# Eight column pairs by seven products instead of five, with low halves made by an adding DMA queue

## The chip, the cores and the metric

The kernel runs on one core of one Trainium2 chip. The metric is the device time of one execution in microseconds (us). A core has TensorE (PE, matrix products; PEld is its loading of weights, which overlaps), VectorE (DVE), ScalarE (ACT), GpSimd (POOL) and SyncE (SP), each with its own list of instructions that it works off in order, and 16 DMA engines that the engines' queues feed. Data are worked on in SBUF (on-chip memory) and products are gathered in PSUM banks.

## The reference

One layer over a sequence of 512 frames of width 1024, in fp32: attention in two branches, a gated mix, and a gated feed-forward layer with a convolution. The change touches only the last:

```python
def conv_glu(x, w_up, conv_w, conv_b, w_down):
    hid = x @ w_up                                  # (512 x 1024) @ (1024 x 5632)
    hid = depthwise_causal_conv(hid, conv_w) + conv_b   # width 3, per column
    gate, up = hid[..., :D_FF], hid[..., D_FF:]     # D_FF = 2816
    return (jax.nn.silu(gate) * up) @ w_down        # (512 x 2816) @ (2816 x 1024)
...
    x = x + mixed @ w_out[l]
    x = x + conv_glu(rms_norm(x, norm2_g[l]), w_ffn_up[l], ffn_conv_w[l], ffn_conv_b[l], w_ffn_down[l])
```

## The kernel before

**High and low halves.** TensorE takes rounded fp32 (type fp32r) here. Each operand is therefore split: ACT copies it into a rounded tile, the high half, and DVE subtracts that from the source, which gives the low half. A product is three matmuls: high by high, high by low, low by high.

**The up projection.** The 2816 gate columns and the 2816 up columns go in 22 *column pairs* `up0` to `up21`: 128 gate columns and the 128 up columns that they gate, 1024 KB of weights each (tile `raw_up`). `run_chunk` runs one pair's matmuls and, at each `yield` between them, one step of the split of the next pair's weights (`split_gen`). At the end of that split stands the load two pairs ahead, on SP's queue. The order of one engine's instructions is set by a scheduler; the function `behind` fixes an order by hand where one is wanted.

An ordinary column pair (`up_body`) is 48 matmuls with 512 columns of tokens. A *seven-product pair* (`up_seven`; the set `SEVEN`, five pairs before) sees the weights as 2 by 2 blocks (gate or up, upper or lower half of the 1024 inputs) and the tokens as 2 by 2 blocks too (left or right half of the sequence), and makes 7 products of such blocks where 8 would be needed: 84 matmuls with 256 columns. It needs sums of weight blocks (`block_sums`, DVE, in tile `sx`), their high and low halves (tiles `wxh`, `wxl`; `split_seven`), and sums of token blocks, which are made once and kept in the four buffers `ts`. Products are put together on DVE and ACT in tiles `hg`, `hu` and `pc`.

After its matmuls, a pair goes through the convolution (`conv`: one ACT instruction, two DVE ones, L851 to L854), the gate (tile `cg`) and the multiplication (L928), which leaves 128 rows of hidden values in `ub`. `ub` has four slots, one for each of four consecutive pairs.

**The operands of the down projection.** It also goes by seven products, over *operand pairs*: hidden rows of column pairs 2i and 2i+1. `pair_sums(i)` makes the sums of blocks (tile `st`, one buffer, and in place in `ub`), then `halves` rounds (L908) and subtracts (L909) them into `ax{i}` (four blocks, high and low, 128x2048) and `ay{i}` (three blocks, 128x1536). Operand pairs 0 to 8 are made inside the up projection, right after the second column pair of each. The `ax` stay in SBUF (eight buffers, pair 8 in a `ts` buffer). The `ay` of pairs 0 to 6 are written to device memory (`ayd`, L933) and read back (`fetch`, L953), both by POOL's DMA queue: five reads after column pair 18, two more in the first steps of the down projection.

**The down projection.** Two passes. The first (`dn0`, 11 steps, one per operand pair) makes products 1, 2, 5 and 7 with 24 matmuls a step. The second (`dn1`, 9 steps) makes products 6, 3 and 4 with 18. Each step's weights come by one load (L123, 1024 KB, then 512 KB), are summed and split by DVE and ACT (`split_down`, L145 to L149), and stand in the same `raw`, `whi` and `wlo` buffers as in the up projection.

Of the kernel before, what the change touches and what calls it, by code (L numbers as in the profile page):

```python
# [8 lines left out]
F32 = mybir.dt.float32  # L9
# [53 lines left out]
SEVEN = (5, 8, 11, 14, 17)  # L63
# [3 lines left out]
def block_kernel(ctx: ExitStack, tc: tile.TileContext, x, xt, params, g2, rbx, wts, wd0, wd1, out):  # L67
# [45 lines left out]
    def load(i, parts=1):  # L113
# [6 lines left out]
        if i >= FIRST_DN:  # L120
            n = i - FIRST_DN
            if n < NP:
                SP.dma_start(raw, wd0[n])  # L123
            else:
                late["load"] = (SP.dma_start(raw[:, 0:1024], wd1[n - NP]),)
            yield
            return

        cuts = [0, *parts, 8] if isinstance(parts, tuple) else [8 * j // parts for j in range(parts + 1)]
        for a, b in zip(cuts, cuts[1:]):  # L130
            sl = slice(256 * a, 256 * b)
            SP.dma_start(raw[:, sl], wts[i, :, sl])
            yield
# [54 lines left out]
    def split_seven(i, raw, hi, lo):  # L188

        key = order[i]  # L190
# [3 lines left out]
        sx = late["sx"]  # L194
        for j, (h, l, src) in enumerate(((hi[:, 0:1024], lo[:, 0:1024], raw[:, 0:1024]),
                                         (wh[:, 0:1024], wl[:, 0:1024], sx[:, 0:1024]),
                                         (hi[:, 1024:2048], lo[:, 1024:2048], raw[:, 1024:2048]),
                                         (wh[:, 1024:1536], wl[:, 1024:1536], sx[:, 1024:1536]))):
            A.copy(h, src)
            V.tensor_tensor(l, src, h.bitcast(F32), op=ALU.subtract)  # L200
            if j < 3:
                yield
# [62 lines left out]
    ayd = dram.tile([7, P, 1536], F32, tag="ayd", name="ayd")  # L265

# [354 lines left out]

    def soft_b(h, t, ps):
# [247 lines left out]
    def pair_sums(i):  # L870
# [5 lines left out]
        if i < 8:  # L876
            ax = fp.tile([P, 2048], F32R, tag="ax", name=f"ax{i}", bufs=8)
            ay = fp.tile([P, 1536], F32R, tag="ay", name=f"ay{i}")
        elif i == 8:

            ax = fp.tile([P, 2048], F32R, tag="ts", name=f"ax{i}", bufs=4)
            ay = fp.tile([P, 1600], F32R, tag="wxh", name=f"ay{i}")[:, 0:1536]
            keep[0] = fp.tile([P, S], F32, tag="hg", name="t2_0")
# [367 lines left out]
```

## Time and profile before

| what | value |
|---|---|
| time, 3 runs | 726.23 us median, 725.83 to 727.21 |
| profiled execution: its own time | 726.66 us |
| profiled execution: span from first to last instruction | 724.9 us |
| TensorE clock granted | 1.000 |
| bytes moved by DMA | 100.91 MB, 139 GB/s |
| up projection with what follows, until the down matmuls | 360.00 to 615.80 us: PE 255.80 busy, DVE 214.60, ACT 138.99 |
| down projection | 615.80 to 724.90 us: PE 104.91 busy, DVE 89.27, ACT 45.90 |

In the rows of groups and of the chain, "L998" is a line of the program, then come the engine, the operation, the written tile, "<-", the tiles read, and "x84" the number of instructions. In a table of stretches each row has its window in us, its length, and busy us with counts for PE, PEld, DVE, ACT and POOL. In the rows of DMA issues the last number is the median time from issue to landing in us. SPq and POOLq are the queues that SP and POOL feed.

### The profile page before, as it was taken

Reading aid. Unit: us, or ns where it says so; the run is one execution under the profiler, and the core shown is the slowest. Engines: PE = TensorE matmul, PEld = TensorE weight load, DVE = VectorE, ACT = ScalarE, POOL = GpSimd, SP = SyncE. Lnnn points to the kernel's source line nnn. Section 1 sums busy time; section 2 is a strip of 40 time slices with the busy share of each in tenths; the row PEclk is TensorE's granted clock in tenths of the full one; section 3 lists DMA queues with packets and bytes.
Section 4 is the critical chain, followed back from the end, with each engine's and each line's share of the span. In section 5 each row is a group of like instructions: output and inputs, shape, how many; then the busy total and the mean of one; then the engine's idle time right before and its main releaser. Section 6 shows DMA issues by size and latency. Waiting matters only on the chain.

```text
span 724.9 us, 10589 instructions
## 1 busy us (share of the span) xinstructions
PE 718.6 (99%) x4019; PEld 627.5 (87%) x4019; DVE 565.4 (78%) x1030; ACT 401.5 (55%) x727; POOL 53.6 (7%) x95
## 2 busy tenths in 40 slices
PE   8999999999999999999999999999999999999997
PEld 8999998888988888888889889889898988888886
DVE  6678867775988888566275799998979985997686
ACT  6675656657767676442254556655545653543541
POOL 2701200000101011000012000000000100000000
PEclk9999999999999999999999999999999999999999
DMA  8632232211313111314536613544335553564563
GB/s 308 250 131 78 83 117 74 74 59 58 118 63 113 59 59 59 136 68 144 195 149 239 203 62 156 186 135 160 118 145 186 181 184 117 173 243 174 177 222 116
DMA packets 24786, 100.91 MB, mean 139 GB/s; under 512 B 2592, under 2 KB 7328, under 8 KB 17184
## 3 DMA queue, kind: packets, MB, share of 16 engines
q1 hardware_dynamic: 21792, 87.00, 33.8%
q0 software_dynamic: 2656, 13.11, 5.0%
q8 instruction: 31, 0.51, 0.3%
q14 instruction: 19, 0.16, 0.1%
q10 hardware_dynamic: 288, 0.14, 0.1%
HBM read 88.44 MB, written 11.80 MB: 138 GB/s over the span
## 4 chain that ended last, share of the span: by engine, by line
PE 98%; DMA 1%; SPq 0%; DVE 0%; ACT 0%; DVEq 0%; issue 0%
PE P L1087 14%; PE p L998 7%; PE pg L254 4%; PE pg L253 4%; PE pg L255 4%; PE pu L254 4%; PE pu L255 4%; PE pu L253 4%; PE qkB L255 2%; PE gB L255 2%; PE qkB L253 2%; PE gA L253 2%; PE gA L254 2%; PE gB L253 2%; PE gA L255 2%; PE qkB L254 2%
## 5 line engine op out<-in xcount | busy, mean ns | idle before, releaser
L253 PE MATMUL pg<-hth,whi_up 128*128 128x512 f32 (+1 forms) x152 | 55.7, 367 | 0.0
L255 PE MATMUL pg<-hth,wlo_up 128*128 128x512 f32 (+1 forms) x152 | 55.7, 366 | 0.0
L254 PE MATMUL pg<-htl,whi_up 128*128 128x512 f32 (+1 forms) x152 | 55.7, 366 | 0.0
L254 PE MATMUL pu<-htl,whi_up 128*128 128x512 f32 (+1 forms) x152 | 55.6, 366 | 0.0
L253 PE MATMUL pu<-hth,whi_up 128*128 128x512 f32 (+1 forms) x152 | 55.6, 366 | 0.0
L255 PE MATMUL pu<-hth,wlo_up 128*128 128x512 f32 (+1 forms) x152 | 55.6, 365 | 0.0
L1087 PE MATMUL P<-whi_dn,ax 128*128 128x512 f32 x176 | 54.4, 389 | 0.0
L149 ACT CAST whi_dn<-raw_dn 128x1024 fp32r<-128x1024 f32 x33 | 34.3, 1051 | 25.5 <-PE P L1087 15.2
L145 DVE TENSOR_TENSOR wlo_dn<-raw_dn,whi_dn 128x1024 fp32r<-128x1024 f32 x33 | 40.0, 1224 | 9.2 <-ACT whi_dn L149 9.1
L228 DVE TENSOR_TENSOR wlo_up<-raw_up,whi_up 128x1024 fp32r<-128x1024 f32 (+1 forms) x40 | 41.2, 1062 | 7.0 <-ACT whi_up L226 7.0
L226 ACT CAST whi_up<-raw_up 128x1024 fp32r<-128x1024 f32 (+1 forms) x40 | 34.5, 917 | 14.7 <-PE pu L254 7.9
L1087 PE MATMUL P<-whi_dn,ay 128*128 128x512 f32 x132 | 40.8, 389 | 0.0
L1087 PEld LDWEIGHTS P<-whi_dn,ax 128*128 128x128 f32 x176 | 33.0, 188 | 6.8
L1087 PE MATMUL P<-wlo_dn,ax 128*128 128x512 f32 x88 | 34.2, 389 | 0.0
L254 PEld LDWEIGHTS pu<-htl,whi_up 128*128 128x128 f32 x152 | 28.6, 188 | 4.7
L253 PEld LDWEIGHTS pu<-hth,whi_up 128*128 128x128 f32 x152 | 28.5, 188 | 4.7
L255 PEld LDWEIGHTS pg<-hth,wlo_up 128*128 128x128 f32 x152 | 28.6, 188 | 4.7
L255 PEld LDWEIGHTS pu<-hth,wlo_up 128*128 128x128 f32 x152 | 28.5, 188 | 4.6
L253 PEld LDWEIGHTS pg<-hth,whi_up 128*128 128x128 f32 x152 | 28.6, 188 | 4.6
L254 PEld LDWEIGHTS pg<-htl,whi_up 128*128 128x128 f32 x152 | 28.6, 188 | 4.5
L633 DVE TENSOR_TENSOR_SCAN aB<-aB,reset 128x127 f32<-128x127 f32 (+3 forms) x32 | 26.0, 817 | 6.7 <-ACT aB L628 6.7
L1087 PEld LDWEIGHTS P<-whi_dn,ay 128*128 128x128 f32 x132 | 24.8, 188 | 5.1
(303 smaller groups left out, 2240.3 us busy)
## 6 DMA issues: line engine op xcount, KB each, us to landing
raw_up<-in_wts SPq DMA_DIRECT2D x22, 1024.0 KB, 4.8
raw_dn<-in_wd SPq DMA_DIRECT2D x11, 1024.0 KB, 4.8
raw_dn<-in_wd SPq DMA_DIRECT2D x11, 512.0 KB, 3.4
ayd<-ay POOLq DMA_DIRECT2D x7, 768.0 KB, 5.2
ay<-ayd POOLq DMA_DIRECT2D x7, 768.0 KB, 6.5
raw_gA<-in_wts SPq DMA_DIRECT2D x4, 1024.0 KB, 4.7
raw_qkB<-in_wts SPq DMA_DIRECT2D x4, 1024.0 KB, 4.8
raw_gB<-in_wts SPq DMA_DIRECT2D x4, 1024.0 KB, 4.7
```

The costliest lines, as they stand in the source:

```text
L145: chain("halves", V.tensor_tensor(o, x, y, op=op))
L149: chain("casts", A.copy(hi[:, sl], src))
L226: A.copy(hi[:, sl], raw[:, sl])
L228: E.tensor_tensor(lo[:, sl], raw[:, sl], hi[:, sl].bitcast(F32), op=ALU.subtract)
L253: PE.matmul(ps, sh, mh, start=first, stop=False)
L254: PE.matmul(ps, sh, ml, start=False, stop=False)
L255: PE.matmul(ps, sl, mh, start=False, stop=last)
L633: V.tensor_tensor_scan(ar, ar, reset[:, S - n:S - 1][:, ::-1], 1.0, op0=ALU.mult, op1=ALU.max)
L998: PE.matmul(ps, st, mv[:, k, :], start=first and k == 0 and n == 0, stop=last and k == 3 and n == 2, skip_group_check=True)
L1087: chain("products", PE.matmul(dst, st, mv, start=first and n == 0, stop=last and n == 2, skip_group_check=True))
```

## The change

1. `SEVEN` has eight pairs, 5, 8, 10, 12, 14, 16, 18 and 20, instead of 5, 8, 11, 14 and 17.
2. The block sums of a seven-product pair need one tile of their own, `s1` (128x512) instead of `sx` (128x1536); two of the sums are written over the weights they were made from. Their splitting goes in another order.
3. For operand pairs 0 to 8 the low halves are made without DVE: ACT writes the rounded value, then the negated rounded value into the low half, and a POOL DMA adds the source to it (`accum_op`), four such DMAs per operand pair.
4. The steps of `pair_sums` aren't issued at the end of the column pair but one at a time at the next yields, from the list `late["todo"]`.
5. `ay` has two buffers. Its spill goes on SP's queue, behind the latest load of weights, a period of two column pairs later than before; `ax0` is spilled too, at operand pair 6, and read back by POOL after column pair 20 into a `ts` buffer. Operand pair 8 uses the ordinary buffers `ax` and `ay`.
6. The reads of `ay` go into the down projection: after steps 0, 2, 3, 5, 6 and 8 of its first pass and after step 0 of its second. Each waits for the landing of the latest load of weights (`after`).
7. `pc` is a third as wide; two PSUM copies go into halves of `hg` and `hu` instead.

```diff
-SEVEN = (5, 8, 11, 14, 17)
+SEVEN = (5, 8, 10, 12, 14, 16, 18, 20)
...
     def block_sums(i):
         b = raws[i].rearrange("p (b c) -> p b c", c=512)
-        sx = late["pool"].tile([P, 1536], F32, tag="sx", name=f"sx_{order[i]}")
-        late["sx"] = sx
-        s1, s2, s4 = (sx[:, 512 * j:512 * (j + 1)] for j in range(3))
+        s1 = late["s1"] = late["pool"].tile([P, S], F32, tag="s1", name=f"s1_{order[i]}")
         V.tensor_tensor(s1, b[:, 1], b[:, 3], op=ALU.add)
         yield
-        V.tensor_tensor(s2, s1, b[:, 0], op=ALU.subtract)
-        yield
-        V.tensor_tensor(s4, b[:, 2], s2, op=ALU.subtract)
-        yield
         V.tensor_tensor(b[:, 1], b[:, 0], b[:, 1], op=ALU.subtract)
         yield
...
+        def part(h, l, c0, src):
+            sl = slice(c0, c0 + src.shape[-1])
+            A.copy(h[:, sl], src)
+            V.tensor_tensor(l[:, sl], src, h[:, sl].bitcast(F32), op=ALU.subtract)
+        part(hi, lo, 0, raw[:, 0:1024])
+        V.tensor_tensor(b[:, 0], s1, b[:, 0], op=ALU.subtract)
+        yield
+        part(wh, wl, 0, s1)
+        part(wh, wl, 512, b[:, 0])
+        yield
+        part(hi, lo, 1024, raw[:, 1024:2048])
+        V.tensor_tensor(b[:, 2], b[:, 2], b[:, 0], op=ALU.subtract)
+        yield
+        part(wh, wl, 1024, b[:, 2])
...
         for _ in body(*splits.pop(key)):
             next(sp, None)
+            if late.get("todo"):
+                late["todo"].pop(0)()
             yield
...
+    def after(ins, others):
+        for o in others:
+            tc.add_manual_dep(ins.ins, o.ins.name, mybir.DependencyInfo(
+                mybir.DependencyClass.Sync, mybir.DependencyReason.DATA), reason="paced")
+        return ins
...
                 A.copy(a[:, sl], src)
-                ins.append(V.tensor_tensor(a[:, n + o:n + sl.stop], src, a[:, sl].bitcast(F32), op=ALU.subtract))
+                if i < 9:
+                    A.activation(lo, src, AF.Copy, scale=-1.0)
+                    G.dma_start(lo, src, accum_op=ALU.add)
+                else:
+                    ins.append(V.tensor_tensor(lo, src, a[:, sl].bitcast(F32), op=ALU.subtract))
...
-            for step in pair_sums(j // 2):
-                step()
-            if j // 2 < 7:
-                G.dma_start(ayd[j // 2], pairs[j // 2][1].bitcast(F32))
+            i = j // 2
+            late["todo"] += pair_sums(i)
+            if 0 < i < 8:
+                late["todo"].append(lambda: behind(SP.dma_start(ayd[i - 1], pairs[i - 1][1].bitcast(F32)), late["ld"]))
+            if i == 6:
+                late["todo"].append(lambda: behind(SP.dma_start(axd, pairs[0][0].bitcast(F32)), late["ld"]))
...
-        G.dma_start(ay, ayd[i])
+        after(G.dma_start(ay, ayd[i]), late["ld"])
...
-        if j == 18:
-            for i in range(5):
-                fetch(i)
+        if j == SEVEN[-1]:
+            keep[0] = fp.tile([P, S], F32, tag="hg", name="t2_0")
+            ax0 = fp.tile([P, 2048], F32R, tag="ts", name="ax0_", bufs=4)
+            G.dma_start(ax0, axd)
+            pairs[0] = (ax0, None)
...
+            n = ({0: 0, 2: 1, 3: 5, 5: 6, 6: 2, 8: 3}, {0: 4})[s].get(i)
+            if n is not None:
+                fetch(n)
```

**How the order changes on DVE.** Before, around the splitting of seven-product pair 11 while pair 10 runs. The numbers in the names of tiles are the pair's and then the program's own; L228 is the low half of an ordinary pair's weights, L200 that of a seven-product pair's, L909 the low half of a down operand, L899 to L901 its sums, L853 a tap of the convolution.

```order
L228 TENSOR_TENSOR wlo_up10_5119<-raw_up10_4965,whi_up10_5118 128x1024
L909 TENSOR_TENSOR ay3_4972<-ub_4184,ay3_4972 128x256
L899 TENSOR_TENSOR ub_4184<-ub_4184 128x256
L900 TENSOR_TENSOR st3_4973<-st3_4973,ub_4184 128x256
L853 SCALAR_TENSOR_TENSOR cg8_5081<-hg8_4992,par_88,cg8_5081 128x511
L200 TENSOR_TENSOR wxl_up11_5209<-sx_up11_5155,wxh_up11_5208 128x1024
L909 TENSOR_TENSOR ax3_4971<-st3_4973,ax3_4971 128x256
L200 TENSOR_TENSOR wxl_up11_5209<-sx_up11_5155,wxh_up11_5208 128x512
L853 SCALAR_TENSOR_TENSOR ub_4184<-hu8_4993,par_88,ub_4184 128x511
L901 TENSOR_TENSOR st3_4973<-ub_4184,st3_4973 128x256
L909 TENSOR_TENSOR ax3_4971<-ub_4184,ax3_4971 128x768
```

Now, from the last product of seven-product pair 12, while pair 14 is split (L1037 and L1038 put products together, L906 is a sum of operand pair 5, L863 and L864 are taps, L192 a low half of pair 14's weights, L194 and L200 block sums):

```order
L1037 TENSOR_TENSOR hu12_5429<-p7_12_5425,hu12_5429 128x256
L906 TENSOR_TENSOR st5_5447<-ub_4185,st5_5447 128x256
L1038 TENSOR_TENSOR hu12_5429<-hu12_5429,pc12_5427 128x256
L863 SCALAR_TENSOR_TENSOR cg12_5538<-hg12_5428,par_88,cg12_5538 128x511
L864 SCALAR_TENSOR_TENSOR cg12_5538<-hg12_5428,par_88,cg12_5538 128x510
L192 TENSOR_TENSOR wlo_up14_5576<-raw_up14_5415,whi_up14_5575 128x1024 x2
L194 TENSOR_TENSOR raw_up14_5415<-s1_up14_5489,raw_up14_5415 128x512
L863 SCALAR_TENSOR_TENSOR ub_4185<-hu12_5429,par_88,ub_4185 128x511
L200 TENSOR_TENSOR raw_up14_5415<-raw_up14_5415 128x512
L864 SCALAR_TENSOR_TENSOR ub_4185<-hu12_5429,par_88,ub_4185 128x510
L192 TENSOR_TENSOR wxl_up14_5578<-raw_up14_5415,wxh_up14_5577 128x512
L939 TENSOR_TENSOR ub_4185<-cg12_5538,ub_4185 128x512
```

The subtractions L909 have gone from this list, and two block sums now stand inside the split, ahead of the last low half.

**On SP's queue**, which had only loads of weights in this stretch, the spills now stand between them:

```order
L129 DMA raw_up17_5684<-in_wts 128x2048
L944 DMA ayd_108<-ay5_5422 128x1536
L947 DMA axd_109<-ax0_4438 128x2048
L129 DMA raw_up18_5850<-in_wts 128x2048
L129 DMA raw_up19_5902<-in_wts 128x2048
L944 DMA ayd_108<-ay6_5639 128x1536
```

A spill follows the load of an odd pair; the next even pair's load stands behind it.

**On POOL's queue**, the end of the list now, the last additions and the reads back:

```order
L918 DMA ay8_6074<-ub_4185 128x256
L918 DMA ax8_6073<-st8_6099 128x256
L918 DMA ax8_6073<-ub_4185 128x768
L918 DMA ay8_6074<-st8_6099 128x512
L1077 DMA ax0__6407<-axd_109 128x2048
L967 DMA ay0_6530<-ayd_108 128x1536
L967 DMA ay1_6613<-ayd_108 128x1536
```

Before, the end of this list held spills and reads alone. Each operand pair now puts four additions on this queue, and the reads of `ay` come after all of them.

More of the change, by code (lines that the diff above doesn't have):

```diff
@@ L121, in load @@
             n = i - FIRST_DN
[L122 to L125, printed above, removed]
+            late["ld"] = (SP.dma_start(raw, wd0[n]) if n < NP else SP.dma_start(raw[:, 0:1024], wd1[n - NP]),)
             yield
@@ L193, in split_seven @@
         splits[key] = tuple(t.rearrange("p (k c) -> p k c", c=P) for t in (hi, lo, wh, wl))
[L194 to L202, printed above, removed]
+        b = raw.rearrange("p (b c) -> p b c", c=512)
+        s1 = late["s1"]
+        def part(h, l, c0, src):
[12 more added lines that the diff above has]
+        part(wh, wl, 1024, b[:, 2])
     def split_gen(i, pieces):
@@ L1023, in body @@
             V.tensor_tensor(hu[:, left], b7, hu[:, right], op=ALU.add)
-            V.tensor_tensor(hu[:, right], hu[:, right], pc[:, 1], op=ALU.add)
+            V.tensor_tensor(hu[:, right], hu[:, right], pc, op=ALU.add)
             up_fin(j, None, hu, g)
@@ L1050, in block_kernel @@
     late["ts"] = token_sums()
+    late["todo"] = []
     for j in range(NF):
@@ L1054, in block_kernel @@
             pass
-        if j == 18:
-            for i in range(5):
-                fetch(i)
+        if j == NF - 1:
+            for step in late["todo"]:
+                step()
+            late["todo"] = []
+        if j == SEVEN[-1]:
[3 more added lines that the diff above has]
+            pairs[0] = (ax0, None)
     BLK = {1: 0, 2: 1, 5: 2, 7: 3, 3: 0, 4: 1, 6: 2}
@@ L1179, in steps1 @@
         for t in range(NT):
-            behind(SP.dma_start(tmp["x"][t // 2][:, t % 2, :], x2d[t]), late["load"])
+            behind(SP.dma_start(tmp["x"][t // 2][:, t % 2, :], x2d[t]), late["ld"])
             if t in (1, 2):
```

29 lines of the change are left out of this document (13 added, 16 removed).

## The prediction

> **What bounds the kernel now.** I read the page's engine shares first, then the chain of work that ended last, then what TensorE waited for, then a table of stretches, then the chain in order of time.
>
> ```profile
> PE 718.6 (99%) x4019; PEld 627.5 (87%) x4019; DVE 565.4 (78%) x1030; ACT 401.5 (55%) x727; POOL 53.6 (7%) x95
> ...
> PE 98%; DMA 1%; SPq 0%; DVE 0%; ACT 0%; DVEq 0%; issue 0%
> ```
>
> PE is 99% busy and 98% of the chain. The waits of PE alone have three rows, all at the program's start; the largest is this one, and the other two are 0.6 and 0.4 us:
>
> ```profile
> PE warm L301 <- DVE warm L298: 1.1, 1, 1.1
> ```
>
> So no later PE instruction waited for data, and the end moves with the PE work, one for one, as long as the other engines keep ahead. How far ahead they are is the question of this change. The table of stretches, cut at the starts of column pairs 5, 8, 14 and 17 (each row is three column pairs; columns are us, then busy us of PE, PEld, DVE, ACT and POOL with counts, clock, DMA share, GB/s):
>
> ```profile
> 435.60:467.28 31.68, 31.68 (x182) 27.92 (x182) 31.68 (x52) 20.01 (x32) 1.07 (x2) 1.00 0.47 176
> ...
> 530.64:562.32 31.68, 31.68 (x182) 27.92 (x182) 26.39 (x41) 16.88 (x26) 1.09 (x2) 1.00 0.49 169
> ```
>
> DVE is busy all of the first stretch and 83% of the last, ACT 53 to 63%, DMA under half; PE never stops. DVE is the engine that would be next. The chain in order of time gives the price of a column pair in both forms:
>
> ```profile
> 467.28 9.89 PE p L998 x84
> 477.17 0.23 PE pg L253
> ...
> 498.96 9.89 PE p L998 x84
> ...
> 615.78 104.94 PE P L1087 x462
> ```
>
> A pair by seven products takes 9.89 us. From 477.17 to 498.96 lie two ordinary pairs: 21.79 us, 10.895 each.
>
> **The change, part by part.** *Products.* Five such pairs become eight. Each new one saves 10.895 - 9.89 = 1.005 us, three save **3.02 us**. PE's list holds nothing else new, and its clock stands at 1.00 in the rows above, so there is no other PE term; the down projection (462 matmuls from 615.78) is the same list. What remains is whether PE stays fed.
>
> *DVE.* From column pair 8 on, seven-product and ordinary pairs alternate, so the load repeats every 9.89 + 10.895 = 20.8 us, where it repeated every 31.68 us. DVE overlaps the end of one instruction with the next, so I take start to start from its timeline:
>
> ```profile
> 482.41 0.42 DVE L909 TENSOR_TENSOR ay<-ub,ay 128x256 fp32r<-128x256 f32 x1
> 482.75 0.42 DVE L899 TENSOR_TENSOR ub<-ub 128x256 f32<-128x256 f32 x1
> ...
> 487.15 0.95 DVE L909 TENSOR_TENSOR ax<-ub,ax 128x768 fp32r<-128x768 f32 x1
> 488.02 0.75 DVE L854 SCALAR_TENSOR_TENSOR cg<-hg,par,cg 128x510 f32<-128x510 f32 x1
> 488.68 0.75 DVE L854 SCALAR_TENSOR_TENSOR ub<-hu,par,ub 128x510 f32<-128x510 f32 x1
> 489.34 2.36 DVE L200 TENSOR_TENSOR wlo_up<-raw_up,whi_up 128x1024 fp32r<-128x1024 f32 x2
> 491.61 0.75 DVE L853 SCALAR_TENSOR_TENSOR ub<-pu,par,ub 128x511 f32<-128x511 f32 x1
> 492.27 0.69 DVE L909 TENSOR_TENSOR ay<-st,ay 128x512 fp32r<-128x512 f32 x1
> 492.87 0.69 DVE L928 TENSOR_TENSOR ub<-cg,ub 128x512 f32<-128x512 f32 x1
> ```
>
> That is 0.34 us at 256 elements, 0.60 at 512, 0.87 at 768, 1.135 at 1024 and 0.66 for a tap of the convolution. In the changed order one 20.8 us period has 8 taps (5.3), 4 of 1024 (4.5), 9 of 512 (5.4) and 9 of 256 (3.1): **18.3 us, 88%**. Before, 31.68 us held 12 taps, 7 of 1024, 9.5 of 512, 1.5 of 768 and 14 of 256: 27.6 us, 87%. The subtractions that leave (0.34 + 0.34 + 0.87 + 0.60 = 2.15 us for each of nine operand pairs) pay for the denser sevens. DVE is no fuller than now, with 2.5 us free in each period.
>
> *Time of a split.* Whether it is also in time: seven-pair 14 is split while 13 runs. By the order shown, after pair 12's last product (call this 0) DVE has the last two 256s, two taps, two 1024s, 512, tap, 512, tap and then 512 four times: 8.6 us. Its handovers with ACT, which rounds the same pieces first, I put at 0.5 to 1 us (the new ACT row of pair sums stands between), so the last low half is ready at about +9.4. PE starts 14 at +10.9 and wants that third only in the sixth product, 5 x 1.41 us later, at +17.9; the first pieces are ready at +5 and wanted at +10.9. Cover: 6 us or more; a delay of DVE up to that costs nothing. The load of the weights of 16 is issued when 14 is split (+9.4), lands 4.8 us later (below) at +14.2, and DVE comes to its first sum at about +15, behind the split of 15, which waits for PE to leave 13 at +10.9. If the load is late by 3 us, DVE idles 2 of its 2.5 free us and PE notices nothing.
>
> *ACT.* It gets a second pass over each operand (scale -1), for which there is no row; the rounding of the same piece is the nearest (groups of ACT in one stretch of the old kernel, each row one shape: busy us, mean ns):
>
> ```profile
> L908 ACT CAST ax<-ub 128x768 fp32r<-128x768 f32 x2 | 1.7, 840 | 0.6 <-DVE ub L899 0.6
> ...
> L908 ACT CAST ay<-st 128x512 fp32r<-128x512 f32 x2 | 1.3, 626 | 0.0
> L851 ACT ACTIVATE ub<-hu,par 128x512 f32<-128x512 f32 x1 | 0.8, 821 | 0.0
> L908 ACT CAST ay<-ub 128x256 fp32r<-128x256 f32 x2 | 0.8, 410 | 0.0
> L908 ACT CAST ax<-st 128x256 fp32r<-128x256 f32 x2 | 0.8, 405 | 0.0
> ```
>
> Between 0.84 + 0.63 + 0.41 + 0.41 = 2.3 us a period (as a cast) and 3.0 (stretched by 821/626, as an activation with pointer operands). I take 2.3, the same pieces. Three shorter roundings and four copies of a seven every 20.8 instead of 31.68 us raise the rest: 53% become about 67%. Hidden under PE; uncovered it would be 2.3 us x 9 = 21 us.
>
> *The adding queue.* Four POOL DMAs per operand pair (128, 128, 384, 256 KB) add the source to the negated high half. No row has such an addition; plain transfers and POOL's own time for one are the nearest rows:
>
> ```profile
> raw_up<-in_wts SPq DMA_DIRECT2D x22, 1024.0 KB, 4.8
> ayd<-ay POOLq DMA_DIRECT2D x7, 768.0 KB, 5.2
> ay<-ayd POOLq DMA_DIRECT2D x7, 768.0 KB, 6.5
> ...
> htd<-xf_n POOLq DMA_DIRECT2D x8, 256.0 KB, 3.3
> ...
> L933 POOL DMA_DIRECT2D ayd<-ay x7 | 3.7, 535 | 134.0 <-DVE ay L909 73.9 <-DVE cg L853 45.9 <-DVE pc L1010 14.2
> ```
>
> POOL pays 0.54 us each and is idle otherwise. An addition takes between 3.3 us (a copy) and twice that, 6.6 (the destination is read too). The last of four is issued when ACT has negated its piece, at about +5.5; the next pair's sums overwrite its source (`st`, one buffer) at about 20.8 - 1.1 = +19.7. Cover 14 us, so I take zero at both ends. Behind a late one stand DVE's sums and then every split; that is rival 1. The Trainium skill (Collectives: The Full Stack, "The bandwidth ceiling: the fold count and why AG ≠ RS ≠ AR") says that an add inside the DMA path costs nothing by its arithmetic but reads two sources, and gives a ratio of 1.93. By it an addition would be 6.4 us by estimate and the sum the same 3.02 us; no run here shows one yet.
>
> *Spills.* They move from POOL to SP, right behind the load of an odd pair's weights, and wait there for additions that were issued a period earlier. Behind a waiting spill stand the loads; by the above there is no wait. Seven of 768 KB and one of 1024 KB in 180 us, 0.47 DMA share at most: hidden. The next user of an `ay` buffer comes 20 us after its spill.
>
> *Fetches.* Five of seven came before the down projection; now the first operand (1024 KB) comes during column pair 21 and six of seven fetches in the first pass, each behind the landing of a load, which is just before the next load is issued. What that does to a load, two places show, with opposite answers (first pair of rows 574 to 580 us, second 631 to 634 us):
>
> ```profile
> ay<-ayd POOLq DMA_DIRECT2D x2, 768.0 KB, 9.0
> raw_up<-in_wts SPq DMA_DIRECT2D x1, 1024.0 KB, 8.8
> ...
> raw_dn<-in_wd SPq DMA_DIRECT2D x1, 1024.0 KB, 4.7
> ay<-ayd POOLq DMA_DIRECT2D x1, 768.0 KB, 7.6
> ```
>
> Behind several fetches the load took 8.8 us, with one fetch issued just after it 4.7: between 0 and 4.0 us more. The tightest use is the load for down step 6:
>
> ```profile
> 637.72 0.33 SPq L123 DMA_DIRECT2D raw_dn<-in_wd  x1
> ...
> 644.73 1.41 DVE L145 TENSOR_TENSOR raw_dn<-raw_dn 128x512 f32<-128x512 f32 x2
> 646.06 2.43 DVE L145 TENSOR_TENSOR wlo_dn<-raw_dn,whi_dn 128x1024 fp32r<-128x1024 f32 x2
> ```
>
> It lands at 637.72 + 4.8 = 642.5, DVE starts on it at 644.73, the first low half is there at about 647.3, and PE comes to it at 615.78 + 6 x 5.45 = 648.5 (24 of the 462 matmuls at 0.227 us are a step). Cover 2.2 + 1.2 = 3.4 us; one fetch beside it I put at up to 2 us, so zero. The Trainium skill (DMA: Bandwidth & Descriptors, "Issuing engines are not separate DMA queues") says that all issuers' transfers interleave on the same 16 engines. By it each load beside a fetch would be slowed, by estimate 1.7 us, still inside the cover; the 8.8 us row agrees and the 4.7 us row does not.
>
> *Sum:* the profiled execution took 726.66 us with a span of 724.9, so 1.76 us lie around it. 726.66 - 3.02 = 723.64; the median of the runs, 726.23, is 0.43 below the profiled one, which makes **723.2**.
>
> **The rivals.** *1. The queue of additions is the bound (slower).* If four additions run one after another, each twice a copy (2 x (3.3 + 3.3 + 3.8 + 3.3) = 27 us, the 384 KB put between the 3.3 and 5.2 rows), a pair takes 27 us of a 20.8 us period. It decides from 20.8 us a pair. `st` is then freed 6.6 us later each time; DVE's 2.5 and PE's 6 us are used up in the first two pairs, and some five pairs remain: 5 x 6.6 - 2 = +31, about 754 us. For it: nothing here shows an addition. Against: three fetches of 768 KB in a row landed in 6.5 to 9.0 us, so transfers of this queue overlap.
>
> *2. Fetches starve the first down pass.* If loads of steps 6, 7, 9 and 10 all take 8.8 us, step 6 is 0.6 us late at PE, step 7 about 1, step 9, which waits for step 7's buffer, 2 to 3: some 4 us, 727 us with the gain in it; half of that gives 725.2. For: the 8.8 us row. Against: that load stood behind four fetches, here there is one.
>
> *3. DVE and ACT are too entangled in the alternating stretch.* Six periods that each run 0.5 us over take the gain back: 726.2. For: the stretch from 435.60, where DVE had no gap at all. Against: PE was fed even there, and the load a period is no larger.
>
> **How the numbers follow.** Forecast 0.72, rival 1 0.07, rival 2 0.12, rival 3 0.09. The likeliest case by itself lies between 722.5 and 724.6. With most of rivals 2 and 3 the range is 722.4 to 726.6; rival 1 is left out. A measurement of this kernel tells 0.2%, 1.5 us, from no change. Faster by more: 0.72 and a small part of 2 and 3, 0.74. Within: the middle of 2 and 3, 0.14. Slower: rival 1 and the far end of 2, 0.12.
>
> **What would show it.** Right: eight stretches of 84 seven-product matmuls of 9.89 us, PE's waits still only at the start, DVE near 88% between column pairs 8 and 20, additions landing within 14 us. Wrong: a PE row waiting for `wlo` or `wxl` in the up projection with DVE waiting for a DMA at the pair sums (rival 1), PE waiting for `wlo_dn` in steps 5 to 10 with loads above 7 us (rival 2), PE waiting behind DVE with no DMA late (rival 3). A seven that takes longer than 9.89 us when it follows an ordinary pair each time would make the gain itself too large.

## The result, and the profile after

The changed kernel takes **731.39 us** (median of 11 runs, 727.48 to 735.97) against 726.14 us before: 1.007 times the time, 95% interval 1.005 to 1.009. It is slower, where 723.2 and faster was forecast. Its runs also lie further apart than those of before (8.5 us against 1.7 us).

The engines' shares and the chain of waits, from the page of the changed kernel:

```profile
PE 718.4 (99%) x4127; PEld 631.6 (87%) x4127; DVE 566.4 (78%) x1035; ACT 427.2 (59%) x789; POOL 81.8 (11%) x125
...
PE 87%; DVE 5%; issue 3%; DMA 2%; ACT 2%; POOL 0%; SPq 0%; DVEq 0%; ACTq 0%; POOLq 0%
```

The chain was 98% PE before. Now 13% of it is something else. What PE waited for (us in total, times, longest):

```profile
PE pg L255 <- DVE cg L864: 1.7, 1, 1.7
PE qA L382 <- ACT whi_qA L226: 1.7, 1, 1.7
PE warm L304 <- DVE warm L301: 1.1, 1, 1.1
PE p L1012 <- ACT hg L1017: 1.0, 1, 1.0
```

The second and third are at the program's start. The first and last are new and lie together, around 475 us, inside column pair 8. The table of stretches shows what follows them (us, then busy us of PE, PEld, DVE, ACT, POOL, granted clock, DMA share, GB/s):

```profile
460.00:480.00 20.00, 17.24 (x98) 15.12 (x97) 15.81 (x24) 13.87 (x24) 3.44 (x4) 0.89 0.67 178
480.00:500.00 20.00, 20.00 (x119) 18.18 (x119) 18.04 (x30) 14.19 (x24) 3.46 (x4) 0.94 0.62 173
477.00:619.00 142.00, 141.96 (x875) 128.57 (x875) 125.57 (x202) 92.77 (x158) 21.29 (x25) 0.98 0.66 189
```

PE stands still for 2.7 us, and around the second gap the clock goes to half for a while: (0.11 + 0.06) x 20 = 3.4 us of clock lost. From 477 us on, DVE is at 125.57 / 142 = 88% and ACT at 65%, as forecast (88 and 67), and PE hardly stops. So one place makes the loss: 726.66 - 3.02 + 2.7 + 3.4 = 729.7 us, and the profiled execution took 729.98. The 3.4 is a little too much, because the half clock begins inside the second gap, where PE does nothing anyway; the matmuls behind it lose 2.9 us (below), and with that some 0.7 us stay unexplained.

The chain in order of time leads back from that place (start, us, what; "issue" is time in which the engine waited for nothing that the profile shows):

```profile
443.36 0.29 POOL ay L918
443.65 7.51 issue
...
451.17 0.86 POOL ax L918
452.03 2.07 issue
454.11 0.85 POOL ax L918
454.96 3.55 issue
458.53 3.93 DMA ay<-st
...
462.58 0.44 DVE st L903
...
465.24 0.95 ACT whi_up L191
...
473.09 1.72 ACT whi_up L226 x2
...
476.26 0.27 ACT hg L1017
476.58 7.17 PE p L1012 x36
```

The part shown begins with the four additions (L918) of operand pair 1. The next pair's first sum (L903) waits for the last of them to land, because it overwrites the tile `st` that the addition reads. Behind that sum, in DVE's and ACT's lists, stand the split of column pair 8 (L191), the rounding of pair 9 (L226) and the copy (L1017) that PE needs for the second half of pair 8. The 36 matmuls after it take 7.17 us, where 36 of an uninterrupted pair take 36 / 84 x 9.89 = 4.24: that is the half clock.

The additions don't overlap. From the records of issue and landing in the changed kernel's trace (us):

| addition | issued | landed | next one issued |
|---|---|---|---|
| ay<-ub, pair 1 | 443.36 | 450.86 | 451.17 |
| ax<-st | 451.17 | 453.80 | 454.11 |
| ax<-ub | 454.11 | 458.22 | 458.53 |
| ay<-st | 458.53 | 462.46 | 462.77 |

Of all 36, not one was issued before the one ahead of it had landed, and 29 of the 35 that follow another were issued 0.31 to 0.35 us after it. One takes 2.6 to 7.6 us, 4.4 on average, so an operand pair's four, from the first issue to the last landing, take 16 to 24 us, 18.6 on average. The program does not ask for this order: none of the semaphore waits that the trace records ahead of these 35 is for the addition before.

### The profile page after: what moved, and what is told of

It is laid out like the page before. It is cut to its first block, busy times and chain, and to the rows that moved or that the text cites. A ratio compares the mean times of both kernels' runs of the same rounds, so it can differ in the third digit from the quotient of the medians.

```text
span 728.2 us, 11018 instructions
## 1 busy us (share of the span) xinstructions
PE 718.4 (99%) x4127; PEld 631.6 (87%) x4127; DVE 566.4 (78%) x1035; ACT 427.2 (59%) x789; POOL 81.8 (11%) x125
## 3 DMA queue, kind: packets, MB, share of 16 engines
q0 software_dynamic: 6976, 16.91, 10.1%
## 4 chain that ended last, share of the span: by engine, by line
PE 87%; DVE 5%; issue 3%; DMA 2%; ACT 2%; POOL 0%; SPq 0%; DVEq 0%; ACTq 0%; POOLq 0%
PE P L1108 14%; PE p L1012 9%; PE pu L255 2%; PE pg L257 2%; PE pu L256 2%; PE pg L255 2%; PE pg L256 2%; PE pu L257 2%; PE qkB L257 2%; PE qkB L255 2%; PE gB L257 2%; PE gA L255 2%; PE gA L256 2%; PE gB L255 2%; PE gA L257 2%
## 5 line engine op out<-in xcount | busy, mean ns | idle before, releaser
L146 ACT CAST whi_dn<-raw_dn 128x1024 fp32r<-128x1024 f32 x33 | 34.5, 1051 | 27.5 <-DMA raw_dn<-in_wd 13.7
L255 PE MATMUL pg<-hth,whi_up 128*128 128x512 f32 (+1 forms) x128 | 46.5, 363 | 1.7 <-DVE cg L864 1.7
L257 PE MATMUL pg<-hth,wlo_up 128*128 128x512 f32 (+1 forms) x128 | 46.4, 362 | 0.0
L256 PE MATMUL pg<-htl,whi_up 128*128 128x512 f32 (+1 forms) x128 | 46.3, 362 | 0.0
L256 PE MATMUL pu<-htl,whi_up 128*128 128x512 f32 (+1 forms) x128 | 46.3, 362 | 0.0
L255 PE MATMUL pu<-hth,whi_up 128*128 128x512 f32 (+1 forms) x128 | 46.3, 362 | 0.0
L257 PE MATMUL pu<-hth,wlo_up 128*128 128x512 f32 (+1 forms) x128 | 46.2, 361 | 0.0
L228 DVE TENSOR_TENSOR wlo_up<-raw_up,whi_up 128x1024 fp32r<-128x1024 f32 (+1 forms) x34 | 33.6, 1030 | 4.2 <-ACT whi_up L226 4.1
L226 ACT CAST whi_up<-raw_up 128x1024 fp32r<-128x1024 f32 (+1 forms) x34 | 28.6, 893 | 9.9 <-PE pu L256 6.3
L645 POOL TENSOR_SCALAR_AFFINE_SELECT bB<-bB 128x128 f32<-128x128 f32 x32 | 13.6, 429 | 149.2 <-DVE bB L644 135.9
L674 ACT CAST pth_A<-pT_A 128x128 fp32r<-128x128 f32 (+2 forms) x40 | 14.6, 371 | 22.4 <-PE pT_A L661 14.7
```

Of the source, the lines that this page charges most:

```text
L146: chain("casts", A.copy(hi[:, sl], src))
L226: A.copy(hi[:, sl], raw[:, sl])
L228: E.tensor_tensor(lo[:, sl], raw[:, sl], hi[:, sl].bitcast(F32), op=ALU.subtract)
L255: PE.matmul(ps, sh, mh, start=first, stop=False)
L256: PE.matmul(ps, sh, ml, start=False, stop=False)
L257: PE.matmul(ps, sl, mh, start=False, stop=last)
```

## The experiments

What follows from each is read from the stages of its profiled execution:

| run | last matmul of kA at | pair 5 to down projection | down projection, first to last matmul | that execution, us | median us |
|---|---|---|---|---|---|
| before | 72.1 | 180.2 | 104.7 | 726.66 | 726.1 |
| changed | 72.0 | 183.5 | 104.8 | 729.98 | 731.4 |
| x9: changed again | 73.8 | 183.1 | 105.1 | 731.64 | 731.6 (one run) |
| x1: copies for additions | 73.9 | 177.0 | 105.7 | 726.33 | 725.9 |
| x2: 8 additions a pair | 72.4 | 260.0 | 104.8 | 806.93 | 812.7 |
| x3: spill behind the load | 72.2 | 189.2 | 105.1 | 736.07 | 733.4 |
| x4: DVE for pairs 0 to 2 | 72.3 | 178.2 | 104.8 | 725.06 | 728.5 |
| x5: five sevens | 71.6 | 185.7 | 105.7 | 732.69 | 733.6 |
| x6: no additions | 73.5 | 178.0 | 107.3 | 728.50 | 727.7 |
| x7: 2 additions | 74.2 | 177.3 | 106.9 | 728.51 | 726.1 |
| x8: 1 addition | 74.1 | 177.8 | 104.8 | 726.78 | 726.7 |
| x10: before, more memory | 71.4 | 180.2 | 104.7 | 725.90 | 725.9 (one run) |
| x11: order of pairs | 73.8 | 184.7 | 104.8 | 733.08 | 730.7 |
| x12: 2 additions, late fetches | 72.5 | 177.3 | 111.2 | 731.17 | 731.2 |
| x13: before, longer list | 72.8 | 199.2 | 104.7 | 751.86 | 751.9 (one run) |
| x14: 2 additions, even fetches | 72.6 | 177.3 | 105.0 | 724.98 | 725.2 |
| x15: as x14, five sevens | 71.6 | 180.2 | 104.7 | 726.75 | 727.2 |

`kA` is the second projection at the start of the program; a matmul counts from its start. "Pair 5" is the first matmul of column pair 5, the first seven-product pair. The profiled execution is not always a typical one: of x2, x4 and x5 it was the fastest, of x3, x7 and x11 the slowest.

The sum expected 180.2 - 3.0 = 177.2 us for the second stage and no change in the others.

### Is it the adding? Copies in its place (x1)

```diff
-                    G.dma_start(lo, src, accum_op=ALU.add)
+                    G.dma_start(lo.bitcast(F32), src)
```

> The changed kernel with the 36 additions turned into plain copies of the same source to the same place on the same queue; the low halves of the down operands then hold the source itself, so the subtraction is left out. The order of TensorE's and the other engines' lists is the same as in the changed kernel. Theory A (an adding DMA is issued only once the addition before it has landed, so four of them take 15 to 22 us a pair and hold the sums and the spills): copies go out 0.5 to 1 us after one another, no wait of DVE for the tile st, TensorE without a gap in column pair 8, 723 to 724 us. Theory B (DVE and ACT are too full and too entangled around column pairs 5 to 8, whatever the queue does): the gap of 2.7 us in pair 8 and the half clock stay, 730 to 732 us.

Measured 725.86 us (724.12 to 727.59), ratio 0.9997 (0.9987 to 1.0007), and the second stage took 177.0 us without a gap. POOL's timeline in this kernel, pair 1:

```profile
444.56 0.54 POOL L918 DMA_DIRECT2D ay<-ub  x1 [10.01 <-DVE hu L1027]
445.22 0.54 POOL L918 DMA_DIRECT2D ax<-st  x1
447.39 0.55 POOL L918 DMA_DIRECT2D ax<-ub  x1 [1.64 <-DVE hg L1033]
450.87 0.54 POOL L918 DMA_DIRECT2D ay<-st  x1 [2.93 <-ACT whi_up L226]
```

The second copy goes out 0.66 us after the first, each takes POOL 0.54 us (an addition 0.86), and from the first issue of four to the last pass 6.3 us, where the additions took 15.2. With the bytes (16.91 MB on this queue), the lists and the spills the same, the gap of pair 8 and the half clock behind it are gone. (The copies also go in fewer packets, 4096 on the queue instead of 6976.) Theory A holds for the stage; the total, 2 us over its forecast, has the two other losses in it that the table shows, one at the start and one in the down projection.

### Twice as many additions (x2)

```diff
-                    G.dma_start(lo, src, accum_op=ALU.add)
+                    h = src.shape[-1] // 2
+                    for q in (slice(0, h), slice(h, 2 * h)):
+                        G.dma_start(lo[:, q], src[:, q], accum_op=ALU.add)
```

> The changed kernel with each addition cut in two halves of the columns, 8 per operand pair; bytes, sums and the order of TensorE's list stay. Theory A: each of the eight takes 2.9 us or more from issue to issue, 24 to 35 us a pair where a period has 20.8, so the queue becomes the bound from the third pair on and the time goes to 745 to 790 us. Theory B: the queue overlaps its transfers and only 36 more issues of 0.9 us are added on POOL, 729 to 733 us.

Measured 812.69 us, ratio 1.118 (1.113 to 1.123): beyond even theory A's range. All 71 that follow another were issued within 0.35 us after its landing, and DVE's waits are the rival's of the prediction, grown large:

```profile
DVE st L903 <- DMA ay<-st: 71.0, 7, 13.9
```

The range was passed because PE, starved pair after pair, also ran 65 us at half clock in that execution.

### Which wait, the spill's or the sums'? (x3, x4)

x3 lets the first spill stand behind the load of column pair 8 on SP:

```diff
             if 0 < i < 8:
+                late["todo"] += [lambda: None] * 2
                 late["todo"].append(lambda: behind(SP.dma_start(ayd[i - 1], ...), late["ld"]))
```

> The changed kernel with the spill of each ay issued two steps later, so that on SP's queue the first spill stands behind the load of column pair 8 instead of ahead of it; the other spills stand where they stood and TensorE's list is the same. Theory A1 (the load of pair 8 is late because the spill ahead of it waits for the last addition of operand pair 0): the load is issued about 2 us earlier and lands 3 to 4 us earlier, DVE's 4.5 us wait for it goes, the gap in pair 8 shrinks below 1 us and the clock stays full: 723 to 726 us. Theory A2 (the wait for the tile st, 2.6 us, makes the gap by itself): the load comes earlier and the gap of 2 to 3 us in pair 8 stays, 729 to 731 us. Theory B: as A2.

Measured 733.42 us, ratio 1.0095 (1.0063 to 1.0127). The load did go out at 439.5 us instead of 443.5, and the stall stayed; three more gaps came between 563 and 587 us. A1 falls. A2's mechanism stands, though the time is above its 729 to 731: in this execution, 736.07 and the slowest of five, DVE waited 18.7 us in all for `st`, against 9.3 in the changed kernel. In x4, which follows, SP still waited 27.5 us for additions ahead of spills, with a second stage of 178.2 us; that wait costs little.

```diff
-                if i < 9:
+                if 3 <= i < 9:
```

> The changed kernel with the low halves of operand pairs 0, 1 and 2 made by DVE subtractions as before, additions only for pairs 3 to 8. Theory A: the pile of additions behind pair 0 is gone, the first spill and the load of pair 8 don't wait, no gap in pair 8 and the additions of pairs 3 to 8 just fit their period: 723 to 725 us. Theory B: DVE gets 2.15 us more for each of three pairs in the stretch where it is too full already, so the gap grows: 731 to 735 us.

Measured 728.53 us (725.06 to 730.45), ratio 1.0026 (1.0007 to 1.0044). The median lies in neither theory's range. In the profiled execution, the fastest at 725.06, the stage is 1 us over the sum, so there the pile behind pairs 0 and 1 was nearly all of the loss. The runs spread over 5.4 us, and by the medians (731.4 in the changed kernel, 728.5 here) only about half of the loss to the forecast of 723.2 went away. That with four additions a pair the other places still go wrong in some executions is likely and not shown, since the one trace is of the fastest.

### Is it the number of sevens, or DVE? (x5, x6)

```diff
-SEVEN = (5, 8, 10, 12, 14, 16, 18, 20)
+SEVEN = (5, 8, 11, 14, 17)
```

> The changed kernel with the old five seven-product pairs (5, 8, 11, 14, 17); additions, spills, fetches and block sums as changed. Theory A (the additions run one at a time, some 18 us an operand pair, and make the loss by themselves): the gap around column pair 8 stays as it stands behind pairs 0 and 1, which are the same here, and the 3.02 us of three sevens are missing: 731 to 736 us. Theory B (it is the eight sevens with their block sums that overfill DVE and ACT): five of them go back to a fed TensorE, 726 to 728 us.

Measured 733.58 us, ratio 1.0104 (1.0084 to 1.0123). With the old set the same two waits stand in the same place, 473 to 477 us:

```profile
PE pg L255 <- DVE cg L864: 1.7, 1, 1.7
...
PE p L1012 <- ACT hg L1017: 1.0, 1, 1.0
```

Theory B falls: the eight sevens are not what makes the loss.

```diff
-                if i < 9:
-                    A.activation(lo, src, AF.Copy, scale=-1.0)
-                    G.dma_start(lo, src, accum_op=ALU.add)
+                if False:
+                    pass
                 else:
                     ins.append(V.tensor_tensor(lo, src, a[:, sl].bitcast(F32), op=ALU.subtract))
```

> The changed kernel with all low halves made by DVE subtractions, no addition on the queue; eight sevens, spills on SP and fetches as changed. DVE gets 2.15 us more a period: 18.3 + 2.15 = 20.5 of 20.8 us. Theory A: no wait for the tile st and no spill that waits for an addition; DVE is at 98 percent and falls behind a little only, 723 to 727 us. Theory B: DVE over its limit, gaps in every second pair, 732 us or more.

Measured 727.71 us, ratio 1.0025 (1.0015 to 1.0035). Its row for the stretch with the alternating pairs:

```profile
477.00:619.00 142.00, 141.07 (x869) 126.66 (x867) 136.11 (x224) 86.00 (x137) 0.55 (x1) 1.00 0.39 138
```

DVE is at 96% without additions, and PE still loses only 0.9 us there. The total is 0.7 us over theory A's range, and most of it lies at the start and in the down projection, where PE waited 1.1 us for DVE's last tap (L864) and 0.7 us for a low half.

### Fewer additions (x7, x8)

```diff
-                if i < 9:
+                if i < 9 and o == 0:                 # x7: the two pieces from ub
+                if i < 9 and o == 0 and n == 1024:   # x8: the piece of 768 columns alone
```

> The changed kernel with only the two pieces that come from ub (768 and 256 columns) made by additions; the two from the tile st go to DVE as before (0.34 + 0.60 = 0.94 us a pair). Theory A: two additions take 7 to 11 us a pair, the tile st is free as soon as DVE is done, spills wait little: TensorE is fed from column pair 5 to 21, 177 us for that stretch, 722.5 to 724.5 us. Theory B (additions in any number disturb the loads, or DVE is too full): 728 us or more.

> As the one with two additions, but only the piece of 768 columns is made by an addition, 1.28 us more on DVE a pair than in the changed kernel (19.6 of 20.8 us). Theory A: as with two, 722.5 to 724.5 us, with the spills, which hold only ay, never waiting for an addition. Theory B: DVE at 94 percent shows gaps, 726 us or more.

Measured 726.12 us, ratio 0.9998 (0.9988 to 1.0009), and 726.72 us, ratio 1.0002 (0.9992 to 1.0011): no change, and both miss theory A's 722.5 to 724.5 us. With two, the second stage is 177.28 us, so the three sevens pay 2.9 of the 3.02 us; the profiled execution lost 2.1 us at the start and 2.2 us in the down projection. It was the slowest of ten, 728.51, so the median has only a part of these losses. PE's waits in it:

```profile
PE qA L382 <- ACT whi_qA L226: 2.0, 1, 2.0
PE warm L304 <- DVE warm L301: 1.1, 1, 1.1
PE P L1108 <- DVE wlo_dn L142: 0.9, 1, 0.9
```

The last one is step 10 of the first down pass. Its load took 8.1 us beside the fetch of `ay2` and 8.4 us for that: the prediction's rival 2, which had this load among the slow ones but counted its delay at steps 6, 7 and 9. With one addition the time fits theory B's 726 us or more, but not for its reason: the second stage is 177.8 us with one gap of 0.4 us, and a start 2 us later than before takes the rest.

### The same kernel again, and the order of the pairs (x9, x11)

> The changed kernel once more, for a second trace. Theory A (additions one at a time, at the edge of their 20.8 us period): the gaps of TensorE between column pairs 5 and 21 come again, in pair 8 or where the queue happened to be late, and the stretch takes 180 to 190 us instead of the 177.2 of the sum; the first additions again leave 0.3 us after the landing of the one before. If TensorE's 1.7 us gap at 6.7 us of the program belongs to the kernel, it is there again; if it is chance, it is between 0.4 and 1.7.

The changed kernel's second trace: 731.64 us, 183.1 us in the second stage, PE gaps of 1.1 and 0.8 us at the start of pair 8 and 0.3 and 1.0 us in its middle, and 29 additions again issued within 0.35 us after a landing. The stall came again, so it belongs to the kernel. The start was 1.7 us later than in its first trace, behind a gap of 2.7 us.

In the changed kernel's TensorE list the scheduler had put two matmuls of pair 9 into the middle of pair 8 (and of pair 17 into 16), and PE's first wait stands at one of them. TensorE's timeline at that place in the changed kernel:

```profile
472.88 0.28 PE L1012 MATMUL p<-ts,wxl_up 128*128 128x256 f32 x1
474.90 0.47 PE L255 MATMUL pg<-hth,whi_up 128*128 128x512 f32 x1 [1.74 <-DVE cg L864]
475.20 0.40 PE L256 MATMUL pg<-htl,whi_up 128*128 128x512 f32 x1
476.58 0.58 PE L1012 MATMUL p<-hth,whi_up 128*128 128x256 f32 x1 [0.97 <-ACT hg L1017]
```

x11 holds an ordinary pair's first matmul behind the last one of the seven ahead (`mm7`):

```diff
+            if k == 0 and "mm7" in late:
+                first7 = late.pop("mm7")
+                behind(PE.matmul(ps[:, c0:c1], hi[:, k, o:o + P], hth[:, k, c0:c1], start=True, stop=False), (first7,))
...
+                continue
```

> The changed kernel with the first matmul of an ordinary column pair held behind the last one of the seven-product pair ahead of it, so that the two matmuls of pair 9 no longer stand in the middle of pair 8 (nor pair 17's in 16). Theory A (the additions): DVE and ACT are late all the same and TensorE waits at the second half of pair 8 for ACT instead; 728 to 733 us. Theory C (TensorE's list is the cause): no gap in pair 8, 723 to 726 us.

Measured 730.69 us, ratio 1.0065 (1.0048 to 1.0083), and the wait is there all the same, now nearly in one piece in pair 8 (3.4 us):

```profile
PE p L1018 <- ACT hg L1023: 4.3, 3, 3.4
```

Theory C falls.

### The late start (x10, x13)

In the eleven traces with eight sevens up to x12, the second piece of the first weights landed late, and PE waited 1.7 to 2.7 us at about 6.7 us; in those of before and x5 it waited at most 1.0. x10 gives the old kernel more device memory, by two unused slots in `ayd` (1.5 MB; the changed kernel has 1 MB more than before); x13 gives it a list for TensorE as long as that of eight sevens:

```diff
+        if (c0, c1) == (0, S) and extra[0] < 108:
+            extra[0] += 4
+            for _ in range(4):
+                PE.matmul(ps[:, c0:c1], hi[:, 0, o:o + P], hth[:, 0, c0:c1], start=True, stop=True)
```

> The kernel before with two more slots in the device memory tensor ayd, which are never used, so that what lies in device memory stands as far apart as with the changed kernel's second spill tensor. If the place in memory makes the slower first loads (landing 5.8 to 6.5 us after issue instead of 4.95), this kernel shows them too and a TensorE gap of 1.7 us or more at the start; if not, gaps of 0.4 and 0.6 us and 726 us.

> The kernel before with 108 matmuls more on TensorE's list (four at the head of each half of the first ordinary column pairs, whose results are overwritten), so that the list is as long as with eight seven-product pairs (4127). They cost 108 x 0.227 = 24.5 us. If the length of TensorE's list (what has to be brought in, or where the program lies) makes the first loads late, TensorE has a gap of 1.7 us or more near 6.7 us and the last matmul of kA comes at 72.5 to 74 us; if not, gaps of at most 1.0 us in all and 71.3 to 72.1 us.

x10: 725.9 us, no wait but the 1.1 us for `warm` that every trace has, kA's last matmul at 71.4 us. x13: 751.86 us, which is 25.7 over before (24.5 for the matmuls), kA's last matmul at 72.8, and the gap is there. TensorE's timeline of before, then of x13:

```profile
7.61 0.74 PE L379 MATMUL qA<-whi_qA,hth 128*128 128x256 f32 x4 [0.59 <-ACT whi_qA L226]
```

```profile
9.21 0.74 PE L379 MATMUL qA<-whi_qA,hth 128*128 128x256 f32 x4 [2.47 <-ACT whi_qA L226]
```

TensorE's list in x13 differs from before's only from 403 us on. Over all traces, the 13 with 4127 matmuls have kA's last one at 72.0 to 74.2 us, 73.1 on average, behind a gap of 1.4 to 2.7 us; the four with 4019 have it at 71.4 to 72.1, 71.7 on average. So a longer TensorE list comes with a start that is some 1.4 us later, and x13, one run, has nothing else that is new. By which path stays open: the queue that brings instructions shows 31 packets with the short list and 32 with the long one (the pages' DMA queues), which may be a sign of it and is no proof.

### Where the fetches go (x12, x14, x15)

All three are x7 with other places for the fetches (and x15 with the old set):

```diff
-            n = ({0: 0, 2: 1, 3: 5, 5: 6, 6: 2, 8: 3}, {0: 4})[s].get(i)
+            n = ({0: 0, 2: 1, 3: 5, 5: 6, 10: 2}, {0: 3, 1: 4})[s].get(i)      # x12
+            n = ({0: 0, 2: 1, 4: 2, 6: 3, 8: 5, 10: 6}, {0: 4})[s].get(i)      # x14, x15
```

> The kernel with two additions a pair, and the fetches of ay2 and ay3 moved from steps 6 and 8 of the first down pass to its last step and to step 0 of the second (ay4 to step 1). Theory: the stretch from column pair 5 to the down projection stays at 177.3 us, the wait of 0.9 us for wlo in step 10 of the first down pass goes and the down projection takes 104.8 us as before instead of 106.9; 723 to 725 us. If the fetches aren't what made that wait, 726 us as with the fetches where they were.

A miss, outside both ranges: 731.23 us, ratio 1.0071 (1.0058 to 1.0085). The wait in step 10 is gone, but the fetches were now too late for the second pass, and one wait with the half clock behind it cost more than it was to save:

```profile
PE P L1108 <- DMA ay<-ayd: 4.7, 1, 4.7
```

> The kernel with two additions a pair and eight sevens, and the fetches spread evenly: after steps 0, 2, 4, 6, 8 and 10 of the first down pass (ay 0, 1, 2, 3, 5, 6) and after step 0 of the second (ay 4), so that two never follow each other within a step and none is late. Theory: column pair 5 to the down projection 177.3 us, down projection 104.8 us, start 0 to 2 us later than before: 723.2 to 725.2 us. If a fetch beside a load is enough to starve a step, the down projection stays at 106 to 107 us and the time at 726.

725.22 us against 726.18 (ratio 0.9991, 0.9982 to 1.0000). The chain in order of time, its column pairs by seven products and the down projection:

```profile
571.79 9.89 PE p L1012 x84
592.59 9.89 PE p L1012 x84
613.39 105.24 PE P L1108 x462
```

Each pair takes 9.89 us, nothing interrupts the down projection, and the only waits of PE in the whole program are the two at its start (1.4 and 1.1 us). This is the fastest of the kernels tried that compute the whole result, by about 1 us, at the edge of what can be told from no change.

> The same with the five seven-product pairs of before. Theory: column pair 5 to the down projection 180.2 us, down projection 104.8 us; if the late start belongs to eight sevens, it is missing here and the time is that of before, 725.6 to 726.6 us; if it belongs to the rest of the change, 727 to 728 us.

727.20 us, ratio 1.0014 (1.0005 to 1.0023). The start (71.6 us) and the two stages are those of before, as expected if the late start belongs to eight sevens. The median by itself would fit the other case (727 to 728), so it is the trace that decides. The profiled execution has 0.5 us more after the last matmul (5.1 instead of 4.6 us), as the others with one or two additions have (x7, x8, x12, x14: 5.0 to 5.1); what makes that stays open.

## Why the prediction was wrong

**The products were right.** A seven takes 9.89 us, and the stage takes 177.28 us in x7, x12 and x14: 2.91 us of the 3.02.

**DVE and ACT were right,** at 88% and 65%; rival 3 (too entangled) falls with x1 and x5.

**The adding queue was the step that failed.** The prediction said: "An addition takes between 3.3 us (a copy) and twice that, 6.6", which was near (2.6 to 7.6), and took the four as overlapping, with "Cover 14 us, so I take zero at both ends". What the runs show in its place: an addition is issued 0.3 us after the one before has landed, so the price of four is their sum, 18.6 us on average of a 20.8 us period, and not the last one's landing alone. The last of the four is issued 13 us after the first on average, where the prediction had it at +5.5 of the period, so the cover of 14 us is mostly used up. The row used against rival 1, three fetches that landed in 6.5 to 9.0 us, was of copies, and copies do overlap here too (x1). The ratio quoted from the Trainium skill (Collectives: The Full Stack, "The bandwidth ceiling: the fold count and why AG ≠ RS ≠ AR"), 1.93, a ratio of two collectives, doesn't describe it either: added and copied (changed kernel and x1, medians to landing), 128 KB from `st` take 2.7 and 2.7 us, 128 KB from `ub` 4.4 and 3.5, 384 KB 4.1 and 2.6, 256 KB 6.2 and 2.3. Rival 1 had the mechanism and the place (DVE waits for `st`) and its price wrong: 27 us a pair instead of 18.6, and a decision "from 20.8 us a pair". At 18.6 us the alternating stretch just holds, and it is the beginning that breaks, where pair 1's additions start right behind pair 0's, beside a load and a spill (443.1 and 443.5 us on SP's queue). That these two slow them is likely and not shown; the first copy in that place took 6.0 us too.

**What a stall costs** was also too small. I priced waits at their length. Here 2.7 us of waiting brought some 3 us more by the half clock.

**Spills:** "by the above there is no wait" fell with the same step: SP waited for additions ahead of its spills, 33.7 us in all between 430 and 600 us. But that cost little, as x3 and x4 show.

**"PE's list holds nothing else new"** overlooked the two matmuls of pair 9 inside pair 8. They did no harm by their place (x11). The list's length did, as far as x13 shows: the later start, which no term of the sum held, costs 1.4 us on average.

**The fetches** at zero held in the changed kernel (104.8 us) and not in kernels whose up projection ran on time (x1 105.7, x7 106.9). x12 and x14 show that their places made it in x7: rival 2's mechanism, about 2 us in its profiled execution, which even spacing takes away. The prediction's 1.7 us for a load beside a fetch comes with no working; in x7 the load of step 10 took 8.1 us, where undisturbed ones take 4.7 to 4.8.

**Together:** the changed kernel's second trace, x9, lies close to the median (731.64 and 731.39 us), and its stages add up to it: 726.66 + 1.7 at the start + 2.9 in the second stage (2.9 gained by the products, 5.8 lost to the additions) + 0.4 in the down projection = 731.7 us.

## What to carry to other kernels

Before work is moved to a queue, find a row that shows that operation twice in a row on that queue: overlap is a property of the kind of transfer, not of the queue. If there is none, price a chain of them by their sum and look first at where several chains meet, not at the steady state. And price a stall of TensorE by what comes after it too.

## What the runs showed of the hardware that was not expected

- An adding DMA isn't issued until the adding DMA before it has landed: smallest distance from landing to next issue 0.31 us over 357 additions in twelve traces, while the same transfers as copies go out 0.66 us apart. The wait shows in no wait row, and no semaphore wait of the program stands for it; POOL's row ends after 0.86 us and the rest is "issue". A plain copy behind an addition does not wait: the read back of `ax0` was issued 1.1 us after the last addition, which landed 6.2 us after its own issue, and in seven other traces a copy behind an addition went out before its landing too.
- TensorE's clock falls to half after gaps shorter than I thought. Two gaps of 1.7 and 1.0 us within 3.4 us brought 6.8 us at half clock (the changed kernel), and a single gap of 2.0 us at the start brought 3.4 us of it in x7 (1.7 us lost), while one of 2.5 us in x13 brought none. The clock records of the traces show what decides. Within a trace, stretches at half clock start whole multiples of 3.41 us apart (in x2 at 445.25, 479.39, 513.52, 554.48 us and later) and, before the program's end, last one to four such steps (where a trace has none inside, I count the steps from the one at its end). In the 17 traces, each of the 19 steps at full clock in which PE was idle for 1.82 us or more was followed by one at half clock, and none with 1.62 us or less was. In x7 the gap fell into one step; in x13 it was cut by the border of two. The Trainium skill (TensorE: Matmul & The Clock Gate, "HAM oscillation — how this bites in real kernels") gives as a rule that there should be no idle gap over about 3.4 us, and in "What's actually happening" that the window of that length runs freely. The traces agree with the second, by the steps of 3.41 us. The first is no safe bound here: 1.82 us idle in one step was enough.
- With TensorE's list 108 matmuls longer, the first loads land later. The second piece of the first weights, issued at 2.2 us in every trace, landed 4.90 to 5.07 us after its issue in the four traces with the short list (4.95 in before) and 5.80 to 6.75 in the 13 with the long one (6.55 in x13).
